# A decoder layer with 32 experts on one core: ScalarE's instructions of the expert loop put into the order in which they are written

## The chip, the core and the metric

The kernel runs on one core of one Trainium2 chip. The metric is device time in microseconds (us) of one execution. Its engines are TensorE (PE; its weight loads are PEld), VectorE (DVE), ScalarE (ACT), GpSimd (POOL) and SyncE (SP), each with an instruction stream of its own; they meet at semaphores. Transfers are issued here by SP (weights, plain loads and stores) and by POOL (indirect gathers and scatters).

## What is computed

One layer over 16 learned tokens and 512 input tokens of width 1024: two mixers in parallel (attention and a state-space scan), gated and added to the residual, then a mixture of 32 experts with a width of 256, of which every token uses two, and a last norm. All is float32. The change lies in the expert part alone:

```python
comb = jnp.sum(jax.nn.one_hot(ids, N_EXPERTS) * w[..., None], axis=1)     # two experts a token
for gi in range(N_EXPERT_GROUPS):
    h = silu(einsum('td,edf->tef', vt, w_gate[sl])) * einsum('td,edf->tef', vt, w_up[sl])
    out = out + einsum('tef,te,efd->td', h, comb[:, sl], w_down[sl])
return rmsnorm(h + out, norm_final)[:, N_META:]
```

## The kernel before

Everything up to about 577 us makes the mixers, the residual `h2` and the routing. Every expert has 64 places for tokens; two experts make a pair `p`, 0 to 15, which fills the 128 rows of TensorE. The expert loop (L1585 on) does for each pair, in the words of the code:

- `expert_gu(p)`: 32 matmuls (L1492) of the gathered tokens `xT` with gate and up weights into one PSUM tile `gu`, then on ScalarE the tanh `th` (L1495), on VectorE two products into `hp`;
- `load_gu`: SP issues the gate and up weights of pair p+3 in four transfers of 1,024 KB (L1038). There are six buffers, one an expert;
- `turn_x(p+1)`: TensorE turns the next pair's gathered rows, VectorE scales them, POOL issues the gather of pair p+4 into `xg` (L1393);
- `expert_h(p)`: TensorE turns `hp`, ScalarE copies it to `hT` (L1508);
- `y_mm`: 16 matmuls (L1528) with the down weights into two PSUM tiles `y`, and `y_split(p, hh)`, one for each half `hh` of the width;
- `load_dn`: SP issues the down weights of later experts (L1047).

`y_split` has two forms. For p below `NP` = 13, ScalarE scales each half of `y` into an SBUF tile `ys` (L1535), and behind the second half POOL scatters the rows of `ys` to a table `yd` in DRAM (L1537). There are two such tiles, used in turn: `ys` of pair p is written over `ys` of pair p-2, so it waits for the landing of that pair's scatter. Each scatter also waits for the landing of the scatter before it, since both write `yd`. For the last three pairs (13, 14, 15) there is no scatter. ScalarE and VectorE cut `y` into a high part `yh` (L1541) and a low part `yl` (L1542), and `combine(p, hh)` adds them to the right tokens with matmuls (L1559). `yh` and `yl` of pair 13 lie in the two tiles of `ys`: `yh` takes that of pair 12, `yl` that of pair 11.

The end of the loop is written out by hand: `combine(13, 0)` stands right behind `y_split(13, 1)` and ahead of `expert_gu(14)` on TensorE. After pair 13's weights, SP issues the last down weights in halves, the gain of the last norm, and eight loads (`load_y`, L1577) that fetch the scattered table `yd` back. POOL adds its two parts (`add_y`, L1580), VectorE adds them to `h2` (L1581), and `sum_h2` (L1569) adds `h2` into the PSUM sums of token blocks 2 and 3.

What sets the order: the program is written out by a scheduler that may move an instruction of an engine past others where the data allow it. `in_order(...)` (L68 on) ties each instruction of the engines that it names to the one before it on the same engine, so these run as written. In the expert loop it names VectorE, TensorE, POOL and SP. ScalarE is left to the scheduler. SP's transfers count on eight completion semaphores in turn, so that each waits for the landing of the transfer eight before it.

Of the kernel before, what the change touches and what calls it, by code (L numbers as in the profile page):

```python
# [72 lines left out]
def hybrid_layer(ctx: ExitStack, tc, A, out):  # L73
    nc = tc.nc
    act, dve, pool, pe = nc.scalar, nc.vector, nc.gpsimd, nc.tensor
# [17 lines left out]
    @contextmanager  # L93
    def in_order(*engines):

        traced = nc.cur_bb.bb.instructions
        n = len(traced)
        yield
        prev = {}
        for i in traced[n:]:  # L100
            if any(i.engine == e.engine for e in engines):
                k = str(i.engine)
                if k in prev:
                    tc.add_manual_dep(i, prev[k], mybir.DependencyInfo(mybir.DependencyClass.NoSync,
                                                                       mybir.DependencyReason.DATA), reason="in_order")
                prev[k] = i.name
# [917 lines left out]
    def load_gu(e, parts=(0, 1)):  # L1024

        if e >= NE:
            return
        i = e % NR
        w = GU_AT[i]
        if i in gus:  # L1030
            pass
        elif w == "u":
            gus[i] = btile(f"gu{i}", n=T)
        else:
            gus[i] = mws[w].tile([128, 4096], F32, tag=f"gu{i}", name=f"gu{i}", bufs=1).rearrange("p (k n) -> p k n", k=KD)
        for h in parts:
            k = slice(h * 4, h * 4 + 4)
            nc.sync.dma_start(gus[i][:, k], A["moe_gu"][e].rearrange("p (k n) -> p k n", k=KD)[:, k])  # L1038
# [419 lines left out]
    def turn_x(p, hh):  # L1458
        if p > 15:
            return  # L1460
        if hh == 0:
            xT[p] = ev.tile([128, KD, 128], F32, tag="xT", name="xT", bufs=1)
        t = xT[p]
        pt = ps("pxT")
        for k in range(4):
            pe.transpose(pt[:, k * 128:(k + 1) * 128], xgs[p % NX][:, (hh * 4 + k) * 128:(hh * 4 + k + 1) * 128], ident)  # L1466
        kk = slice(hh * 4, hh * 4 + 4)
        dve.tensor_mul(t[:, kk], pt.rearrange("p (k n) -> p k n", k=4),  # L1468
                       g_ffn[:, kk, None].to_broadcast([128, 4, 128]))
        if hh == 0:  # L1470
            return
        rh = xgs[p % NX][:, D:D + 1]
        dve.tensor_copy(rsl[:, p:p + 1], rh)
        dve.scalar_tensor_tensor(wsl[:, p:p + 1], wsl[:, p:p + 1], rh, rh, op0=ALU.mult, op1=ALU.mult)
        if p + NX < 16:
            gather(p + NX)

    def expert_gu(p):

        nf = 1 if p < 15 else 2  # L1480
        gu = [ps("gu") for _ in range(nf)]
        th, hp = (ev.tile([128, 256], F32, tag=x, name=x, bufs=n) for x, n in (("th", 1), ("hp", 2)))
        h_[p] = hp
        n = 256 // nf
        for kh in range(2):
            for f in range(nf):
                for k in range(kh * 4, kh * 4 + 4):
                    for e in range(2):
                        r, w = slice(e * 64, (e + 1) * 64), gus[(2 * p + e) % NR][:, k]
                        if nf > 1:  # L1490
                            w = w.rearrange("p (g f n) -> p g f n", g=2, f=nf)[:, :, f]
                        pe.matmul(gu[f][r, :2 * n], xT[p][:, k, r], w, start=(k == 0), stop=(k == KD - 1), skip_group_check=True)  # L1492
                if kh:
                    c = slice(f * n, (f + 1) * n)
                    act.activation(th[:, c], gu[f][:, :n], AF.Tanh, scale=rsl[:, p:p + 1])  # L1495
                    dve.scalar_tensor_tensor(hp[:, c], th[:, c], 1.0, gu[f][:, :n], op0=ALU.add, op1=ALU.mult)  # L1496
                    dve.tensor_mul(hp[:, c], hp[:, c], gu[f][:, n:2 * n])
# [3 lines left out]
    def expert_h(p, fs=(0, 1)):  # L1501
        if 0 in fs:
            hT_[p] = ev.tile([128, 2, 128], F32, tag="hT", name="hT", bufs=1)
        pt = ps("phT")
        for f in fs:
            pe.transpose(pt[:, f * 128:(f + 1) * 128], h_[p][:, f * 128:(f + 1) * 128], ident)
        c = slice(fs[0] * 128, (fs[-1] + 1) * 128)
        act.activation(hT_[p].rearrange("p f n -> p (f n)")[:, c], pt[:, c], AF.Copy)  # L1508

    def y_start(p):  # L1510
        if p < NP:
            y_[p] = ev.tile([128, D], F32, tag="y" + "hl"[p % 2], name="ys", bufs=1)
            return
        if p < 15:
            st = rx.tile([128, T], F32R, tag="rx", name="st")
            r = [ev.tile([128, D], F32R, tag="y" + x, name="y" + x, bufs=1) for x in "hl"]
        else:
            st, *r = (mo.tile([128, D + 1], F32R, tag=f"xg{i}", name=f"yx{i}", bufs=1)[:, :n] for i, n in enumerate((T, D, D)))
        dve.tensor_scalar(st, iot, tokf[:, p:p + 1], None, op0=ALU.is_equal)
        y_[p] = st, *r  # L1520
# [3 lines left out]
    def y_mm(p, f, hh):  # L1524
        if f == 0:
            yp[hh] = ps("y")
        for e in range(2):
            pe.matmul(yp[hh][e * 64:(e + 1) * 64], hT_[p][:, f, e * 64:(e + 1) * 64],  # L1528
                      dns[(2 * p + e) % ND][:, f, hh * 512:(hh + 1) * 512],
                      start=(f == 0), stop=(f == 1), skip_group_check=True)  # L1530
# [17 lines left out]
    def combine(p, hh, blocks=range(4)):  # L1548

        st, yh_, yl_ = y_[p]  # L1550
        c = slice(hh * 512, (hh + 1) * 512)
        for b in blocks:
            kept = b in HB
            on = kept and p > NP or p == 15 and hh
            if kept and p == NP:
                hs[b, hh] = ps("pcl")
            pc = hs[b, hh] if kept else more[b, hh] if on else ps("pc")
            for n, x in enumerate((yh_, yl_)):
                pe.matmul(pc, st[:, b * 128:(b + 1) * 128], x[:, c], start=(n == 0 and not on),  # L1559
                          stop=(n == 1 and (p == 15 or not kept and p < 15 - hh)), skip_group_check=True)  # L1560
            if not kept and p < 15 - hh:
                dve.tensor_add(h2[:, b, c], h2[:, b, c], pc)
            elif not kept:
                more[b, hh] = pc
# [17 lines left out]

    LC = [slice(0, 512), slice(512, 1024)]

    with in_order(dve, pe, pool, nc.sync):  # L1585
        for hh in range(2):
            turn_x(0, hh)
        for p in range(16):
            expert_gu(p)
            for h in range(2):  # L1590
                for e in range(2 * p + NR, 2 * p + NR + 2):
                    load_gu(e, (h,))
            if p < 15:
                turn_x(p + 1, 0)
                turn_x(p + 1, 1)
                if p > NP:
                    combine(p - 1, 1, range(CB))
                expert_h(p)
                if p > NP:
                    combine(p - 1, 1, range(CB, 4))  # L1600
                y_start(p)
                for hh in range(2):
                    for f in range(2):
                        y_mm(p, f, hh)
                    y_split(p, hh)
            else:
                y_start(p)
                add_y(2)
                add_y(3)
                expert_h(p, (0,))  # L1610
                combine(p - 1, 1, (2, 3))
                y_mm(p, 0, 0)
                expert_h(p, (1,))
                y_mm(p, 0, 1)
                for hh in range(2):
                    y_mm(p, 1, hh)
                    y_split(p, hh)
                combine(p - 1, 1, (0, 1))
                sum_h2()
                add_y(0)  # L1620
                add_y(1)
            for e in range(2 * p + ND, min(2 * p + ND + 2, 30)):
                load_dn(e)
            if 2 * p + ND + 1 in (31, 32):
                for c in LC:
                    load_dn(30, [c])
                    load_dn(31, [c])
                nc.sync.dma_start(dns[25 % ND][:, 0], bcast_row(A["g_fin"], D))
            if p == NP:
                for b in (2, 3, 0, 1):  # L1630
                    load_y(b)
            if NP <= p < 15:
                combine(p, 0)
        for b, hh in ((2, 0), (3, 0), (2, 1), (0, 0), (3, 1), (0, 1), (1, 0), (1, 1)):
            combine(15, hh, (b,))
# [181 lines left out]
```

## Time and profile before

| | us |
|---|---|
| three runs, median (lowest to highest) | 854.13 (851.97 to 854.8) |
| the profiled execution | 855.57 |
| its span, first to last instruction | 853.7 |
| TensorE busy | 774.0 |
| VectorE, ScalarE, POOL busy | 412.9, 275.9, 160.6 |

The profiled execution is 1.44 us above the median, and 1.87 us of its time lie outside the span. A row of a timeline gives the start, the duration, the engine, the line, the operation with output and inputs, how many instructions are merged in it (x), and in brackets how long the engine had been idle before and what ended that. Names are those of the program without their numbers. Sums of busy time are averages over stages with different limits; the expert loop is the stretch from 577 us to about 843 us.

### The profile page before, as it was taken

Reading aid. Unit: us, or ns where it says so; the run is one execution under the profiler, and the core shown is the slowest. Engines: PE = TensorE matmul, PEld = TensorE weight load, DVE = VectorE, ACT = ScalarE, POOL = GpSimd, SP = SyncE. Lnnn points to the kernel's source line nnn. Section 1 sums busy time; section 2 is a strip of 40 time slices with the busy share of each in tenths; the row PEclk is TensorE's granted clock in tenths of the full one; section 3 lists DMA queues with packets and bytes.
Section 4 is the critical chain, followed back from the end, with each engine's and each line's share of the span. In section 5 each row is a group of like instructions: output and inputs, shape, how many; then the busy total and the mean of one; then the engine's idle time right before and its main releaser. Section 6 shows DMA issues by size and latency. Waiting matters only on the chain.

```text
span 853.7 us, 11153 instructions
## 1 busy us (share of the span) xinstructions
PE 774.0 (91%) x4122; PEld 523.4 (61%) x4122; DVE 412.9 (48%) x945; ACT 275.9 (32%) x525; POOL 160.6 (19%) x201
## 2 busy tenths in 40 slices
PE   4999999999999999999999999959898887887494
PEld 4999886777788778767665788843333332332252
DVE  4787349865357545666857654261212211121155
ACT  6455333333135542455553424111111100011014
POOL 6100105322011000034435000051111010010042
PEclk9999999999999999999999999978999999999698
DMA  7721234324212241102122955869999999999932
GB/s 279 269 100 57 94 135 137 124 87 162 77 59 99 74 160 59 41 26 63 34 83 92 398 215 187 334 224 220 418 417 420 420 420 421 418 420 418 347 120 99
DMA packets 44445, 175.57 MB, mean 206 GB/s; under 512 B 9776, under 2 KB 14144, under 8 KB 28256
## 3 DMA queue, kind: packets, MB, share of 16 engines
q1 hardware_dynamic: 37808, 160.88, 49.9%
q0 software_dynamic: 5760, 13.71, 4.7%
q8 instruction: 35, 0.57, 0.3%
q10 hardware_dynamic: 816, 0.20, 0.1%
q14 instruction: 26, 0.21, 0.1%
HBM read 163.63 MB, written 15.27 MB: 210 GB/s over the span
## 4 chain that ended last, share of the span: by engine, by line
PE 67%; issue 11%; DMA 10%; DVE 6%; ACT 4%; POOL 0%; POOLq 0%; ACTq 0%; DVEq 0%
DMA yd<-ys,dst 8%; PE gu L1492 6%; PE y L1528 3%; PE pbr L676 3%; PE pbr L674 3%; PE pbr L673 3%; PE po L876 2%; PE ga L241 2%; PE gs L241 2%; PE ga L243 2%; PE ga L242 2%; PE gs L242 2%; PE pout L1093 2%; PE gs L243 2%; PE z L241 2%
## 5 line engine op out<-in xcount | busy, mean ns | idle before, releaser
L1492 PE MATMUL gu<-gu,xT 128*64 128x512 f32 (+1 forms) x544 | 129.7, 599 | 8.8 <-DMA gu<-in_moe_gu_dram 8.6
L1492 PEld LDWEIGHTS gu<-gu,xT 128*64 128x64 f32 x544 | 43.1, 143 | 92.0 <-issue 71.8
L1496 DVE SCALAR_TENSOR_TENSOR hp<-th,gu 128x256 f32<-128x256 f32 (+1 forms) x17 | 6.9, 405 | 188.0 <-ACT th L1495 188.0
L1495 ACT ACTIVATE th<-gu,rsl 128x256 f32<-128x256 f32 (+1 forms) x17 | 7.9, 462 | 180.0 <-PE gu L1492 180.0
L1528 PE MATMUL y<-dn,hT 128*64 128x512 f32 x256 | 58.7, 599 | 7.4 <-ACT hT L1508 7.4
L822 DVE CUSTOM_DVE_ANT_0 sp<-sp,amask 128x144 f32<-128x144 f32 (+4 forms) x80 | 33.9, 459 | 18.0 <-PE sp L814 14.9
L1528 PEld LDWEIGHTS y<-dn,hT 128*64 128x64 f32 x256 | 16.9, 136 | 38.4 <-issue 27.0
L1537 POOL DMA_INDIRECT yd<-ys,dst x13 | 13.1, 1005 | 132.3 <-ACT ys L1535 124.1
L852 PE MATMUL st<-qs,kq 97*128 97x512 f32 (+4 forms) x80 | 28.6, 358 | 1.0 <-DVE kq L797 1.0
L1393 POOL DMA_INDIRECT xg<-vd,idx x16 | 16.3, 1019 | 61.3 <-DMA yd<-ys,dst 33.9
L1466 PEld LDWEIGHTS pxT<-cst,xg 128*128 128x128 f32 x128 | 14.4, 146 | 18.5 <-issue 14.4
L301 POOL TENSOR_TENSOR rfs<-rfm,mhalf 128x4 f32<-128x4 f32 (+1 forms) x5 | 7.6, 1521 | 92.6 <-DVE rfm L300 92.6
L882 POOL TENSOR_TENSOR pw<-pw 128x400 f32<-128x400 f32 x14 | 15.9, 1157 | 43.8 <-PE po L876 43.8
L1468 DVE TENSOR_TENSOR xT<-pxT,pv 128x512 f32<-128x512 f32 x32 | 20.6, 681 | 6.8 <-PE pxT L1466 6.7
L853 PE MATMUL st<-qs,kq 97*128 97x512 f32 (+4 forms) x80 | 23.6, 296 | 0.2 <-DMA qs<-rs 0.2
L1466 PE MATMUL pxT<-cst,xg 128*128 128x128 f32 x128 | 18.3, 289 | 5.8 <-DMA xg<-vd,idx 5.8
L394 DVE SCALAR_TENSOR_TENSOR cacc<-xp,cwh,cacc 128x528 f32<-128x528 f32 x30 | 22.9, 763 | 0.4
L854 PE MATMUL st<-qs,kq 97*128 97x512 f32 (+4 forms) x80 | 23.0, 295 | 0.0
L861 ACT ACTIVATE pw<-st 128x512 f32<-128x512 f32 (+1 forms) x32 | 16.7, 547 | 19.4 <-PE st L857 16.1
L1535 ACT ACTIVATE ys<-y,wsl 128x512 f32<-128x512 f32 x26 | 16.9, 686 | 15.5 <-PE y L1528 15.5
L583 DVE TENSOR_SCALAR lm<-lm,acs 128x128 f32<-128x128 f32 x64 | 19.2, 366 | 2.5 <-DMA lm<-acd 2.5
L882 POOL TENSOR_TENSOR pw<-pw,pb 128x272 f32<-128x272 f32 (+2 forms) x42 | 20.2, 512 | 0.0
(925 smaller groups left out, 2043.9 us busy)
## 6 DMA issues: line engine op xcount, KB each, us to landing
gu<-in_moe_gu_dram SPq DMA_DIRECT2D x64, 1024.0 KB, 22.0
dn<-in_moe_dn_dram SPq DMA_DIRECT2D x30, 1024.0 KB, 21.0
win<-in_win_dram SPq DMA_DIRECT2D x19, 1024.0 KB, 4.7
yd<-bd POOLq DMA_DIRECT2D x2, 2048.0 KB, 12.2
lm<-acd SPq DMA_DIRECT2D x16, 256.0 KB, 3.6
wbs<-in_wbs_dram SPq DMA_DIRECT2D x4, 1024.0 KB, 4.7
wba<-in_wba_dram SPq DMA_DIRECT2D x4, 1024.0 KB, 11.4
wo<-in_wout_dram SPq DMA_DIRECT2D x4, 1024.0 KB
```

The costliest lines, as they stand in the source:

```text
L241: pe.matmul(dst, ah, bh, start=(i == 0), stop=False)
L242: pe.matmul(dst, ah, bl, start=False, stop=False)
L243: pe.matmul(dst, al, bh, start=False, stop=(i == n - 1))
L673: pe.matmul(pb_, wh[:, k], oh[k], start=(k == 0), stop=False)
L674: pe.matmul(pb_, wh[:, k], ol[k], start=False, stop=False)
L676: pe.matmul(pb_, wl[:, k], oh[k], start=False, stop=(k == last))
L822: dve.tensor_tensor_reduce(s_, s_, amask[:, L - nk + n0:L - nk + n1], 1.0, -3.0e38, op0=ALU.add, op1=ALU.max, accum_out=mx[:, n_:n_ + 1])
L852: pe.matmul(d_, kh_[0:97, kb], qh_[0:97, q0:q1], start=True, stop=False)
L882: last_sum[0] = eng.tensor_tensor(x, x, P[b], op=ALU.add)
L1466: pe.transpose(pt[:, k * 128:(k + 1) * 128], xgs[p % NX][:, (hh * 4 + k) * 128:(hh * 4 + k + 1) * 128], ident)
L1492: pe.matmul(gu[f][r, :2 * n], xT[p][:, k, r], w, start=(k == 0), stop=(k == KD - 1), skip_group_check=True)
L1528: pe.matmul(yp[hh][e * 64:(e + 1) * 64], hT_[p][:, f, e * 64:(e + 1) * 64], dns[(2 * p + e) % ND][:, f, hh * 512:(hh + 1) * 512], start=(f ...
```

## The change

The name `act` is added to the list of engines of the one `in_order` around the expert loop.

```diff
-    with in_order(dve, pe, pool, nc.sync):
+    with in_order(act, dve, pe, pool, nc.sync):
         for hh in range(2):
             turn_x(0, hh)
         for p in range(16):
```

Instructions of TensorE, VectorE, POOL and SP stand in the same order in both kernels. On ScalarE, the order is the same for pairs 0 to 4 and from `yh` of pair 13 on; between them the two `ys` of pairs 5 to 12 change places. The first place is ScalarE at pairs 5 to 7 (`th_6093`, `th_6160` and `th_6227` are the tanh of pairs 5, 6 and 7, `ys_6141` the output tile of pair 5), before:

```order
L1495 ACTIVATE th_6093<-gu_6092,rsl_5264 128x256
L1508 ACTIVATE hT_6136<-phT_6137 128x256
L1495 ACTIVATE th_6160<-gu_6159,rsl_5264 128x256
L1508 ACTIVATE hT_6203<-phT_6204 128x256
L1495 ACTIVATE th_6227<-gu_6226,rsl_5264 128x256
L1535 ACTIVATE ys_6141<-y_6142,wsl_5263 128x512
L1535 ACTIVATE ys_6141<-y_6148,wsl_5263 128x512
```

and now:

```order
L1495 ACTIVATE th_6093<-gu_6092,rsl_5264 128x256
L1508 ACTIVATE hT_6136<-phT_6137 128x256
L1535 ACTIVATE ys_6141<-y_6142,wsl_5263 128x512
L1535 ACTIVATE ys_6141<-y_6148,wsl_5263 128x512
L1495 ACTIVATE th_6160<-gu_6159,rsl_5264 128x256
L1508 ACTIVATE hT_6203<-phT_6204 128x256
```

The two `ys` of pair 5 moved from behind the tanh of pair 7 to behind `hT` of pair 5; the pairs 6 to 11 moved in the same way. The second place is ScalarE at pairs 11 to 13 (`ys_6543` and `ys_6606` are those of pairs 11 and 12, `th_6628`, `hT_6664` and `yh_6670` belong to pair 13), before:

```order
L1495 ACTIVATE th_6628<-gu_6627,rsl_5264 128x256
L1535 ACTIVATE ys_6543<-y_6544,wsl_5263 128x512
L1535 ACTIVATE ys_6543<-y_6550,wsl_5263 128x512
L1508 ACTIVATE hT_6664<-phT_6665 128x256
L1535 ACTIVATE ys_6606<-y_6607,wsl_5263 128x512
L1535 ACTIVATE ys_6606<-y_6613,wsl_5263 128x512
L1541 ACTIVATE yh_6670<-y_6673,wsl_5263 128x512
```

and now:

```order
L1535 ACTIVATE ys_6606<-y_6607,wsl_5263 128x512
L1535 ACTIVATE ys_6606<-y_6613,wsl_5263 128x512
L1495 ACTIVATE th_6628<-gu_6627,rsl_5264 128x256
L1508 ACTIVATE hT_6664<-phT_6665 128x256
L1541 ACTIVATE yh_6670<-y_6673,wsl_5263 128x512
```

Between the tanh of pair 13 and `yh` of pair 13 there stood the four `ys` of pairs 11 and 12; now there is `hT` alone, and all `ys` lie ahead.

## Rows read from the trace of the kernel before

**Rows 1.** Chain that ended last, in order of time: start, duration, engine or transfer.

```profile
783.04 8.41 DMA yd<-ys,dst
...
792.23 8.22 DMA yd<-ys,dst
```

**Rows 2.** Timeline of ScalarE in the expert loop.

```profile
646.61 0.69 ACT L1535 ACTIVATE ys<-y,wsl 128x512 f32<-128x512 f32 x1 [1.06 <-PE y L1528]
653.52 0.47 ACT L1495 ACTIVATE th<-gu,rsl 128x256 f32<-128x256 f32 x1 [6.23 <-PE gu L1492]
...
680.12 1.26 ACT L1535 ACTIVATE ys<-y,wsl 128x512 f32<-128x512 f32 x2
...
783.45 1.26 ACT L1535 ACTIVATE ys<-y,wsl 128x512 f32<-128x512 f32 x2
800.55 1.27 ACT L1541 ACTIVATE yh<-y,wsl 128x512 fp32r<-128x512 f32 x2 [15.84 <-DMA yd<-ys,dst]
813.70 0.47 ACT L1495 ACTIVATE th<-gu,rsl 128x256 f32<-128x256 f32 x1 [11.89 <-PE gu L1492]
```

**Rows 3.** Timeline of TensorE in the expert loop, matmuls alone.

```profile
646.36 7.04 PE L1492 MATMUL gu<-gu,xT 128*64 128x512 f32 x32
...
775.70 5.34 PE L1492 MATMUL gu<-gu,xT 128*64 128x512 f32 x14 [1.97 <-DMA gu<-in_moe_gu_dram]
...
783.61 3.65 PE L1528 MATMUL y<-dn,hT 128*64 128x512 f32 x16 [0.53 <-ACT hT L1508]
801.29 0.79 PE L1559 MATMUL pc<-yh,st 128*128 128x512 f32 x1 [14.03 <-ACT yh L1541]
...
805.42 8.23 PE L1492 MATMUL gu<-gu,xT 128*64 128x512 f32 x32
...
820.28 0.50 PE L1559 MATMUL pc<-yh,st 128*128 128x512 f32 x1
...
822.35 7.13 PE L1492 MATMUL gu<-gu,xT 128*64 128x256 f32 x64
...
835.63 3.60 PE L1569 MATMUL pcl<-h,cst 128*128 128x512 f32 x8
```

**Rows 4.** Timeline of POOL in the expert loop.

```profile
647.57 1.01 POOL L1537 DMA_INDIRECT yd<-ys,dst  x1 [2.63 <-ACT ys L1535]
...
681.66 1.00 POOL L1537 DMA_INDIRECT yd<-ys,dst  x1 [23.60 <-ACT ys L1535]
682.96 1.02 POOL L1393 DMA_INDIRECT xg<-vd,idx  x1 [0.30 <-issue]
...
792.23 0.98 POOL L1537 DMA_INDIRECT yd<-ys,dst  x1 [8.19 <-DMA yd<-ys,dst]
814.38 9.79 POOL L1580 TENSOR_TENSOR gu<-gu,gu 128x1024 f32<-128x1024 f32 x4 [21.16 <-PE pxT L1466]
```

**Rows 5.** Waits of SP's queue, at 791.5 to 792.5, then at 804 to 805.

```profile
SPq L1047 <- DMA gu<-in_moe_gu_dram: 2.7, 1, 2.7
...
SPq L1577 <- DMA gu<-in_moe_gu_dram: 1.8, 1, 1.8
```

**Rows 6.** Timeline of VectorE behind the last pair.

```profile
830.85 2.35 DVE L1581 TENSOR_TENSOR h<-h,gu 128x1024 f32<-128x1024 f32 x2
834.57 1.61 DVE L1542 SCALAR_TENSOR_TENSOR yx<-y,wsl,yx 128x512 fp32r<-128x512 f32 x2 [1.38 <-ACT yx L1541]
...
841.60 0.16 DVE L1655 SCALAR_TENSOR_TENSOR fq<-fq 128x1 f32<-128x1 f32 x1 [3.15 <-ACT gu L1651]
```

**Rows 7.** Stretches: length; PE, PEld, DVE, ACT, POOL busy; granted clock; DMA share; GB/s.

```profile
680.00:784.00 104.00, 87.44 (x358) 31.04 (x358) 15.68 (x43) 14.31 (x29) 13.07 (x13) 0.95 1.02 420
...
802.00:806.00 4.00, 3.94 (x10) 2.45 (x11) 2.12 (x4) 0.00 (x0) 0.00 (x0) 0.50 0.92 312
```

**Rows 8.** The page: POOL's queue (packets, MB, share) and its two plain blank fills.

```profile
q0 software_dynamic: 5760, 13.71, 4.7%
...
yd<-bd POOLq DMA_DIRECT2D x2, 2048.0 KB, 12.2
```

## The prediction

> **What bounds the kernel now.** I read the stretches first, then the chain that ended last, then the timelines of the engines around its longest step. From 680 to 784 us the transfers run at 420 GB/s with a DMA share of 1.02 [rows 7]: this part of the expert loop goes at the pace of the weights, and TensorE shows waits of some 2 us for them, as the 1.97 us ahead of the second half of pair 13's gate and up matmuls [rows 3]. A ScalarE that does the same work in another order can give nothing there. The end of the loop is different. TensorE finishes pair 13's `y` at 783.61 + 3.65 = 787.26 and then sits idle for 14.03 us, until 801.29, waiting for `yh` of ScalarE [rows 3]. No weight load is named there. ScalarE itself had been idle for 15.84 us, waiting for a scatter [rows 2], and the chain runs through two scatters in a row, 8.41 us from 783.04 and 8.22 us from 792.23 [rows 1]. The second could not start before the first had landed: POOL waited 8.19 us for it [rows 4]. Everything behind, to the end of the kernel, hangs on this.
>
> Why are two scatters left at 783? In the early pairs, ScalarE writes `ys` straight behind `y`: the second half of pair 4 at 646.61, its scatter leaves at 647.57 [rows 2, 4]. For pair 5 it waits behind the tanh of pair 7: 680.12, scatter at 681.66, and POOL had stood idle for 23.60 us, the gather behind it too, at 682.96 [rows 2, 4]. From there on, each scatter is about two pairs late, and no one notices, since nothing reads the table. At pair 13 someone does: `yh` and `yl` are written over the tiles of pairs 12 and 11, so all scatters must have landed. The two last ones, each late, now come one behind the other.
>
> **The change part by part.** (1) *Eight pairs of `ys` move up.* No work is added: 16 instructions keep their duration, 1.26 us a pair [rows 2]. In the new place they stand ahead of the next pair's tanh. That is a possible new wait: behind a `ys` that waits, tanh and `hT` queue on ScalarE, and behind those all of TensorE. The early pairs already have this order and show its cost. The second `ys` of pair 4 ends at 647.30, the next tanh starts at 653.52 because of TensorE, after 6.23 us of idleness [rows 2]. So the cost on the path is 0, hidden by seven microseconds of gate and up matmuls (7.04) [rows 3]; without that cover it would be 1.26 a pair, 10 us for eight.
>
> (2) *Eight scatters and the gathers behind them leave earlier*, by about 681.66 - (647.57 + 13.1) = 21 us at first; 13.1 is my estimate of the distance of two early pairs on TensorE (7.04 for gate and up, 3.65 for `y` [rows 3], some 2.4 for the turns and the two short waits between them). Their bytes do not change, but they move ahead of weights in a full pipe. POOL's queue moved 13.71 MB, of which the two blank fills are 4.2; the other 9.5 over 29 gathers and scatters give at most 0.33 MB each [rows 8], or 0.8 us at 420 GB/s [rows 7]. When pair 13's last weights land, two more scatters than before may have passed: 1.6 us. For pair 14's it is one, 0.8 us; for all that comes later none, the bytes are the same by then. The bounds are 0 and 1.6; I take 1.6, since the pipe is full.
>
> (3) *The wait of 14.03 us goes. What is late next?* Pair 13's `y` ends at 787.26 + 1.6 = 788.9. `yh` follows it at once, as for pair 14, where the matmuls of `combine` start at 820.28 and the next pair's at 822.35: 2.07 us [rows 3]. So pair 14's gate and up matmuls start at 790.9 instead of 805.42. Their weights: SP's transfer at 791.8 had waited for a landing of such weights, which is the last of pair 14's, since each transfer waits for the eighth before it [rows 5]; with the 0.8 it is 792.6, and the second half of the matmuls wants them at 790.9 + 3.5 = 794.4. They take 7.04 us as in the early pairs rather than 8.23 [rows 3], and end at 797.9 instead of 813.65: **15.75 us gained**. The 8.23 and the 4.13 us of `combine` (805.42 - 801.29) were run after the idle time, with a granted clock of 0.50, the lower level of 1.2 GHz, at 802 to 806 [rows 7]. If the clock is low again, these cost 1.19 + 2.06 = 3.3 us of the gain; I take the short ones, since TensorE works without a gap of that size now.
>
> (4) *The rest of the tail moves along, if its transfers are there.* Pair 15's matmuls start 8.70 us after pair 14's end (822.35 - 813.65 [rows 3]): 806.6. The last gate and up weights landed by 804.9 [rows 5]: no wait. `sum_h2` would come at 835.63 - 15.75 = 819.9 [rows 3]. It needs the fetched table, and these loads do not move, as they stand behind the weights on SP. POOL added them from 814.38 on, four in 9.79 us [rows 4]; the row names TensorE as what ended the wait, but those loads are issued after 802 and land about then, so I let POOL start at 814.4 again. Its second sum is ready at 819.3, VectorE's two adds (1.2 us each [rows 6]) at 820.5. The first two of the eight `sum_h2` matmuls (0.45 each) do without them and end at 820.8: just in time. The fourth sum is ready at 824.2, on VectorE at 825.4; the norm's first step, 841.60 before [rows 6], would want VectorE at 825.85. Both margins are under half a microsecond, so I take off 0.5: **15.3 us**.
>
> The profiled execution would go from 855.57 to 840.3; it lies 1.44 above the median of the runs shown, and from that median, 854.13, I get 838.8.
>
> **What the Trainium skill says on two of these steps.** On (1), "PSUM — Partial Sum Buffer", section "Engine vs sequencer instructions", says that ScalarE's queue is strictly first in, first out: a `ys` that waits for its scatter holds all behind it. The trace agrees: the `yh` at 800.55 held ScalarE for 15.84 us [rows 2]. By that rule alone, fixing the order can lose; it is the second rival. On (2), "DMA: Bandwidth & Descriptors", section "Issuing engines are not separate DMA queues", says that transfers of SP and POOL share the same 16 engines and interleave, so an earlier scatter is paid by weights; by that rule (2) is 1.6 us rather than 0, which the DMA share of 1.02 bears out [rows 7].
>
> **The rivals.** *The transfers hold the tail.* The gain of 15.3 uses nearly all the slack that the fetched table has. If its loads land 5 us later than before (SP issues them behind transfers that wait for landings of weights), POOL, VectorE and `sum_h2` move by 5, and the time is 843.3; with the low clock of (3) on top of a smaller slip it is about the same. Against it: the bytes ahead of them are the same by then, and one scatter less runs beside them. *ScalarE is held by its own order (slower).* `ys` of pair p needs the landing of pair p-2's scatter. From that issue (647.57 for pair 4) to `ys` two pairs later there are about 26 - 1.7 = 24 us, and 6.2 more until the tanh behind it would start. It decides once a scatter takes over 30 us from issue to landing: at 33 us, six pairs (7 to 12) lose 3.3 each, 20 us, and with the 15.3 won back the kernel ends near 859. Against it: scatters took 8.2 to 8.4 in the fullest stretch [rows 1]. *The wait stays.* If the last scatter lands near 800 whenever it is issued, because the weights crowd it out, the time is 854.1. Against it, the same 8.2 us.
>
> **How the numbers follow.** The forecast has 0.77, the late transfers 0.14, the wait that stays 0.05, the slower case 0.04. The likeliest is the forecast, 838.8. It spans 836.0 (no shift in (2), where the fetched table caps the gain at 16.2, less 2 us, as far as the lowest run lies below the median) to 842.1 (low clock); I carry the range to 845.0 to take in the late transfers. About 0.3%, 2.6 us, is what a measurement of this kernel can tell from no change: faster by more 0.91, within 0.05, slower 0.04.
>
> **What would show it.** Right: in the new timelines each second `ys` follows its `y` within a microsecond, all 13 scatters are issued before 772, `yh` of pair 13 waits for TensorE alone, the idle time ahead of pair 13's `combine` falls below 1 us, pair 14's tanh starts near 798, and POOL's sums still start near 814. Wrong: a `ys` that waits for a transfer, TensorE waiting for weights ahead of pair 14 or 15 for more than 2 us, or VectorE's adds ahead of `sum_h2` waiting for POOL. The forecast fails most easily at (4), at the fetched table.

## The result and the profile after

The changed kernel takes 844.58 us (median of 4 runs, 842.84 to 846.47), beside 853.40 for the kernel before (4 runs, 851.97 to 854.80; three of them are those of the table above). The ratio is 0.9897, with an interval of 0.9863 to 0.9931: it is 0.7 to 1.4% faster. The forecast was 838.8 with a range of 836.0 to 845.0. The time lies inside the range, at its far end: of the 15.3 us that were promised, about 9 came. The profiled execution took 846.47, its span 844.7 instead of 853.7: 9.0 us less. It is the longest of the four, but a second profile of this kernel (experiment 8, an execution of 844.43 us) shows the same wait at the end.

The big wait is gone. This is the timeline of ScalarE of the changed kernel around pair 13 (start, duration, engine, line, operation, count; in brackets the idle time before it and what ended it):

```profile
770.93 0.69 ACT L1535 ACTIVATE ys<-y,wsl 128x512 f32<-128x512 f32 x1 [2.06 <-PE y L1528]
772.65 0.69 ACT L1535 ACTIVATE ys<-y,wsl 128x512 f32<-128x512 f32 x1 [1.03 <-PE y L1528]
786.45 0.69 ACT L1541 ACTIVATE yh<-y,wsl 128x512 fp32r<-128x512 f32 x1 [2.09 <-PE y L1528]
797.51 0.47 ACT L1495 ACTIVATE th<-gu,rsl 128x256 f32<-128x256 f32 x1 [8.70 <-PE gu L1492]
```

The two `ys` of pair 12 end at 773.34, ten microseconds before the place where the last two stood in [rows 2], and `yh` of pair 13 waits for TensorE alone; in [rows 2] it waited 15.84 us for a scatter. The timeline of POOL:

```profile
660.03 1.00 POOL L1537 DMA_INDIRECT yd<-ys,dst  x1 [2.63 <-ACT ys L1535]
...
773.61 0.99 POOL L1537 DMA_INDIRECT yd<-ys,dst  x1 [16.49 <-ACT ys L1535]
...
815.61 11.41 POOL L1580 TENSOR_TENSOR gu<-gu,gu 128x1024 f32<-128x1024 f32 x4 [41.01 <-PE y L1528]
```

Pair 5's scatter leaves at 660.03, before at 681.66, and the last of the thirteen at 773.61, before at 792.23 [rows 4]. But look at the last row: the four sums of the fetched table take 11.41 us where they took 9.79. TensorE, matmuls alone, shows both what was won and what was given back:

```profile
784.42 3.65 PE L1528 MATMUL y<-dn,hT 128*64 128x512 f32 x16 [0.53 <-ACT hT L1508]
788.00 0.50 PE L1559 MATMUL pc<-yh,st 128*128 128x512 f32 x1
...
790.07 7.36 PE L1492 MATMUL gu<-gu,xT 128*64 128x512 f32 x32
...
806.13 7.13 PE L1492 MATMUL gu<-gu,xT 128*64 128x256 f32 x64
...
819.41 1.02 PE L1569 MATMUL pcl<-h,cst 128*128 128x512 f32 x2
824.87 5.35 PE L1569 MATMUL pcl<-h,cst 128*128 128x512 f32 x6 [4.43 <-DVE h L1581]
```

Pair 14's gate and up matmuls start at 790.07 instead of 805.42, pair 15's at 806.13 instead of 822.35, and `sum_h2` at 819.41 instead of 835.63 [rows 3]: 16.2 us won. Then comes a row that was not there before: six of the eight `sum_h2` matmuls wait 4.43 us for an add of VectorE, and take 5.35 us, where all eight took 3.60 [rows 3]. This wait stands in the chain that ended last (start, duration, engine, tile, line), where no POOL sum and no VectorE add of the fetched table stood before:

```profile
815.61 2.34 POOL gu L1580
...
818.04 3.41 POOL gu L1580
...
821.47 3.35 DVE h L1581
...
824.87 5.35 PE pcl L1569 x6
```

The account: 16.2 won up to `sum_h2`, of which 9.0 arrived in the span. The other 7.2 went between there and the norm. VectorE's first norm step (L1655) starts 5.97 us after the start of `sum_h2` in [rows 3] and [rows 6] (841.60 - 835.63), and now at

```profile
832.59 0.16 DVE L1655 SCALAR_TENSOR_TENSOR fq<-fq 128x1 f32<-128x1 f32 x1 [3.35 <-ACT gu L1651]
```

which is 13.18 us after it: 7.2 lost, 4.43 of them by the wait and 2.8 by the slower matmuls behind it. From the norm to the end of the span it is 12.1 us in both kernels.

### The profile page after: what moved, and what is told of

It reads as the page before. It is cut to its first block, busy times and chain, and to the rows that moved or that the text cites. A ratio compares the mean times of both kernels' runs of the same rounds, so it can differ in the third digit from the quotient of the medians.

```text
span 844.7 us, 11164 instructions
## 1 busy us (share of the span) xinstructions
PE 772.8 (91%) x4122; PEld 523.0 (62%) x4122; DVE 413.9 (49%) x945; ACT 277.6 (33%) x525; POOL 162.7 (19%) x201
## 4 chain that ended last, share of the span: by engine, by line
PE 71%; DMA 17%; DVE 5%; ACT 4%; issue 1%; POOL 1%; SPq 0%; ACTq 0%; DVEq 0%; POOLq 0%
DMA gu<-in_moe_gu_dram 11%; PE gu L1492 8%; PE y L1528 4%; DMA dn<-in_moe_dn_dram 3%; PE pbr L673 3%; PE pbr L676 3%; PE pbr L674 3%; PE po L876 2%; PE ga L241 2%; PE gs L241 2%; PE ga L243 2%; PE ga L242 2%; PE gs L242 2%; PE gs L243 2%; PE pout L1093 2%; PE pout L1094 2%
## 5 line engine op out<-in xcount | busy, mean ns | idle before, releaser
L1492 PE MATMUL gu<-gu,xT 128*64 128x512 f32 (+1 forms) x544 | 127.0, 585 | 10.9 <-DMA gu<-in_moe_gu_dram 10.9
```

## The experiments

**Theory.** The four last sums collide: POOL's sums and VectorE's adds work on tiles in the same memory at the same time and hold each other up, and through `sum_h2` this costs TensorE 4.4 us and some clock. **Rivals:** the fetched table itself comes too late for the early `sum_h2`; or the gain at pair 13 is smaller than read and the 7 us have another source. For the gain there is the theory that the wait for two late scatters was all there was to win, and the rival that the earlier scatters of all eight pairs have a worth or a price of their own.

**1. The changed kernel with POOL's sum of the fetched table moved to VectorE.** VectorE then does eight adds in a row, and none of them can meet one of POOL's.

```diff
     def add_y(b):
-        pool.tensor_tensor(ya[b, 0], ya[b, 0], ya[b, 1], op=ALU.add)
+        dve.tensor_add(ya[b, 0], ya[b, 0], ya[b, 1])
         dve.tensor_add(h2[:, b], h2[:, b], ya[b, 0])
```

> The changed kernel, with POOL's four sums of the fetched table moved to VectorE. Theory (POOL and VectorE slow each other when both add whole rows at once; that is what delays the second sum of h2): VectorE's adds take 1.2 us each again, the one that the sum of h2 waits for ends near 820.5 instead of 824.8, TensorE's wait of 4.4 us shrinks below 1 us, its clock stays up, and the time falls by 4 to 6 us below the changed kernel, to 838.5 to 841 (before: 853.4). Rival (the fetched table simply lands too late): the wait stays at 3 us or more and the time stays near 844.6.

It took 840.3 us (839.54 to 841.12, 4 runs), beside 855.01 for the kernel before: ratio 0.9819, interval 0.9803 to 0.9836. The intervals of this version and the changed kernel lie apart; it is the best of all here, and beats both kernels. Its VectorE:

```profile
816.77 1.23 DVE L1580 TENSOR_TENSOR gu<-gu,gu 128x1024 f32<-128x1024 f32 x1 [0.87 <-DMA gu<-yd]
818.03 1.23 DVE L1581 TENSOR_TENSOR h<-h,gu 128x1024 f32<-128x1024 f32 x1
819.20 1.23 DVE L1580 TENSOR_TENSOR gu<-gu,gu 128x1024 f32<-128x1024 f32 x1
820.46 1.23 DVE L1581 TENSOR_TENSOR h<-h,gu 128x1024 f32<-128x1024 f32 x1
```

and its TensorE:

```profile
820.60 3.98 PE L1569 MATMUL pcl<-h,cst 128*128 128x512 f32 x8
```

Every add takes 1.23 us, the one that POOL did in 2.4 included. The eight matmuls run in one piece, and TensorE needs 7.7 us from `sum_h2` to its last matmul, close to the 7.3 of before. The gain, 14.7 us by the medians and 15.5 by the ratio (855.01 times 0.0181), is about what the forecast had promised for the order alone.

**2. The changed kernel with the fetched table's loads issued ahead of the load of `g_fin`.**

```diff
                     load_dn(30, [c])
                     load_dn(31, [c])
-                nc.sync.dma_start(dns[25 % ND][:, 0], bcast_row(A["g_fin"], D))
             if p == NP:
                 for b in (2, 3, 0, 1):
                     load_y(b)
+                nc.sync.dma_start(dns[25 % ND][:, 0], bcast_row(A["g_fin"], D))
```

> The changed kernel, with the load of the last norm's gain issued behind the eight loads of the table instead of ahead of them; its issue took 4.05 us. Theory (late table plus collision): the first table loads are issued 4 us earlier, near 799, the fourth about 1.4 us earlier (it waits for a landing of weights), POOL's first sum starts near 812, TensorE's wait of 4.4 us falls to 2 or 3, the time to 841 to 843. Rival (the table's landing has no part in it, POOL is released by TensorE as its row says): POOL still starts at 815.6 and the time stays near 844.6.

It took 845.76 (844.45 to 845.96; ratio 0.9887, 0.987 to 0.9903), which can't be told from the changed kernel, and the edit mostly missed. On SP's queue of the changed kernel, then of this one:

```profile
799.09 4.05 SPq L1628 DMA_DIRECT2D dn<-in_g_fin_dram  x1
803.25 9.88 SPq L1577 DMA_DIRECT2D gu<-yd  x8
```

```profile
798.99 12.74 SPq L1577 DMA_DIRECT2D gu<-yd  x8
812.70 0.33 SPq L1631 DMA_DIRECT2D dn<-in_g_fin_dram  x1
```

The first of the eight loads is issued 4 us earlier, but the 4 us that the issue of `g_fin` took stayed at that place of the queue. The view of L1577 gives the shortest, the median and the longest of the eight issues in ns:

```profile
L1577 SPq DMA_DIRECT2D gu<-yd x8: 319/320/4002, 799.0 to 811.4; - x8
```

The longest, 4.0 us, is the first, so the second load leaves at 803.08; in the changed kernel none took over 0.52 us. Why an issue takes 4 us at that place was not looked into. POOL's first sum needs both of the first two loads. So it starts at 814.18 instead of near 812, between the 815.61 of the changed kernel's first profile and the 813.90 of its second (experiment 8):

```profile
814.18 11.49 POOL L1580 TENSOR_TENSOR gu<-gu,gu 128x1024 f32<-128x1024 f32 x4 [39.89 <-DMA gu<-yd]
```

This row names what ends POOL's wait, the landing of the table, where the rows of the changed kernel and [rows 4] name TensorE. The sums still take 11.49 us, VectorE's first two adds 6.67 where 2.35 would do [rows 6], and the matmuls of `sum_h2` still wait, 0.83 and 2.16 us:

```profile
816.79 6.67 DVE L1581 TENSOR_TENSOR h<-h,gu 128x1024 f32<-128x1024 f32 x2 [2.24 <-POOL gu L1580]
```

```profile
820.24 1.13 PE L1569 MATMUL pcl<-h,cst 128*128 128x512 f32 x2 [0.83 <-DVE h L1581]
...
823.52 4.54 PE L1569 MATMUL pcl<-h,cst 128*128 128x512 f32 x6 [2.16 <-DVE h L1581]
```

So the table has its part in the wait: TensorE was ready for `sum_h2` at 819.4 in both kernels, and POOL's start, 1.4 us earlier than in the first profile, took 1.4 us off the wait (2.99 in all instead of 4.43). The 3 us that are left are there although POOL starts where the forecast had it. What a table that is there 5 us earlier would do stays untried.

**3. The kernel before with ScalarE tied to program order from pair 11 on.** The late scatters of pairs 5 to 8 stay late; only those of the end move.

```diff
+        tied = ExitStack()
         for p in range(16):
+            if p == 11:
+                tied.enter_context(in_order(act))
...
+        tied.close()
```

> The kernel before, with ScalarE tied to its written order only from pair 11 on; pairs 5 to 10 keep their late output copies. Theory (the whole gain is the wait at pair 13): as the changed kernel, 843 to 846, no idle time of 14 us ahead of pair 13's combine. Rival (earlier scatters and gathers along the loop help too): less than half of the gain, 849 or more.

It took 846.91 (844.6 to 848.19; ratio 0.9904, 0.9885 to 0.9924): 0.9 us above the expected span, but by its ratio, 0.9904 beside 0.9897, the whole gain of the change as far as the intervals can tell. Its POOL,

```profile
681.78 1.00 POOL L1537 DMA_INDIRECT yd<-ys,dst  x1 [23.59 <-ACT ys L1535]
...
775.12 0.99 POOL L1537 DMA_INDIRECT yd<-ys,dst  x1 [8.38 <-DMA yd<-ys,dst]
```

is late at pair 5 as in [rows 4] and 17 us ahead of [rows 4] at pair 12 (775.12, before 792.23). What the change does to pairs 5 to 8 has no worth and no price that can be measured here.

**4. The kernel before with tiles of their own for pair 13's `yh` and `yl`.** The order stays, and the scatters stay late; what goes is the reason to wait for them, since these two tiles are now those of gathered rows that are no longer needed.

```diff
-            r = [ev.tile([128, D], F32R, tag="y" + x, name="y" + x, bufs=1) for x in "hl"]
+            r = [mo.tile([128, D + 1], F32R, tag=f"xg{i}", name=f"yg{i}", bufs=1)[:, :D] for i in (1, 2)] if p == NP else [ev.tile([128, D], F32R, tag="y" + x, name="y" + x, bufs=1) for x in "hl"]
```

> The kernel before, ScalarE's order untouched, with the high and low parts of pair 13 in two gather tiles that are free by then instead of the tiles of the output copies: pair 13 no longer waits for the scatters of pairs 11 and 12. Theory (the wait for the scatters is the cause, the order only what made them late): combine of pair 13 starts near 788 with the scatters as late as before (issued near 783 and 792), and the time is that of the changed kernel, 843 to 846. Rival (late scatters cost in another way too, for example as they hold back the table's loads): 848 or more.

It took 846.6 (845.22 to 847.96; ratio 0.989, 0.987 to 0.9911): the same gain once more. Its scatters are as late as before, and its `combine` does not care:

```profile
783.61 1.00 POOL L1537 DMA_INDIRECT yd<-ys,dst  x1 [14.49 <-ACT ys L1535]
792.77 1.00 POOL L1537 DMA_INDIRECT yd<-ys,dst  x1 [8.16 <-DMA yd<-ys,dst]
```

```profile
787.76 1.19 PE L1559 MATMUL pc<-yg,st 128*128 128x512 f32 x4
```

Here too `sum_h2` waits 4.45 us for VectorE, so that wait belongs to the earlier tail, and not to ScalarE's order.

**5. The kernel before with the sums on VectorE**, the edit of experiment 1 without the change.

> The kernel before, ScalarE's order untouched, with POOL's four sums of the fetched table moved to VectorE. Theory (the collision of POOL and VectorE exists only where the tail has moved up on them; before, POOL had ended at 824.2 and VectorE began at 830.85): nothing to win here, VectorE takes 4.9 us for the first two blocks instead of 2.35, all hidden or up to 1.5 us lost, ratio to before 0.999 to 1.002. Rival (VectorE is simply the better engine for these sums, whatever the order): a gain of 3 us or more here too, ratio 0.996 or less.

855.63 us (852.43 to 857.3, 10 runs) beside 856.04 for the kernel before: ratio 1.0 (0.9975 to 1.0025), nothing. Its TensorE still waits at pair 13:

```profile
802.89 0.79 PE L1559 MATMUL pc<-yh,st 128*128 128x512 f32 x1 [14.07 <-ACT yh L1541]
```

The collision of the sums costs nothing as long as the tail comes 16 us later. Each of the two edits was looked at alone: the order gives about 9 us, the sums 0, and both together about 15.

**6. The changed kernel with one tile for `ys` in place of two**, so that each `ys` needs the landing of the scatter just before it. This halves the room of the slower rival.

```diff
-            y_[p] = ev.tile([128, D], F32, tag="y" + "hl"[p % 2], name="ys", bufs=1)
+            y_[p] = ev.tile([128, D], F32, tag="y" + "h", name="ys", bufs=1)
```

> The changed kernel, with one tile for the output copies instead of two, so that each waits for the scatter of the pair just before it. Theory (the written order has room: a scatter lands 8.4 us after its issue, and the next pair's copy comes at least 12 us after it): no copy waits for a scatter, time as the changed kernel, 842 to 847. Rival (ScalarE is held by its own order as soon as the room shrinks): copies wait for landings, tanh and TensorE behind them, 850 or more.

846.95 us (843.34 to 848.31; ratio 0.9895, 0.9841 to 0.9949), as the changed kernel. All 26 waits of `ys` are for TensorE, none for a scatter; the row (waiting instruction, releaser: us in all, times, longest) reads the same in both:

```profile
ACT ys L1535 <- PE y L1528: 40.2, 26, 2.2
```

**7. The changed kernel, where POOL and VectorE take turns once.** POOL's third sum is written over the tile that VectorE's second add reads, and so starts only when that add is done. Nothing else changes; POOL's first and second sums stand as they were.

```diff
-        pool.tensor_tensor(ya[b, 0], ya[b, 0], ya[b, 1], op=ALU.add)
-        dve.tensor_add(h2[:, b], h2[:, b], ya[b, 0])
+        o = ya[b or 3, 0]; pool.tensor_tensor(o, ya[b, 0], ya[b, 1], op=ALU.add)
+        dve.tensor_add(h2[:, b], h2[:, b], o)
```

> The changed kernel, with POOL's third sum (block 0) made to wait until VectorE's add of block 3 is done, by writing it over a buffer that this add reads. Theory (POOL and VectorE cannot run these two-input operations at the same time, the later one waits for the whole of the earlier one): VectorE's add of block 3 takes 1.2 us instead of 3.35, TensorE's wait falls from 4.4 to about 2.3 us, the time by 1 to 3 us below the changed kernel, ratio about 0.002 lower. POOL's second sum stays stretched to 3.4 us, since it still meets VectorE's add of block 2. Rival (VectorE's add is slow there for another reason, such as the fetched rows landing at that time): it stays at 3 us or more, the time too.

**8. The changed kernel again**, beside 7 on the same chip.

> The changed kernel itself, beside the others on the same chip, for the comparison: ratio to before about 0.990, TensorE idle for some 4.4 us ahead of the sum of h2, VectorE's add of block 3 near 3.35 us.

VectorE's two adds in the changed kernel, in the first profile:

```profile
818.00 1.22 DVE L1581 TENSOR_TENSOR h<-h,gu 128x1024 f32<-128x1024 f32 x1 [3.28 <-POOL gu L1580]
821.47 3.34 DVE L1581 TENSOR_TENSOR h<-h,gu 128x1024 f32<-128x1024 f32 x1 [2.25 <-POOL gu L1580]
```

the second of them in experiment 8, and TensorE's wait for it there:

```profile
819.75 3.35 DVE L1581 TENSOR_TENSOR h<-h,gu 128x1024 f32<-128x1024 f32 x1 [2.23 <-POOL gu L1580]
```

```profile
823.15 5.02 PE L1569 MATMUL pcl<-h,cst 128*128 128x512 f32 x6 [4.45 <-DVE h L1581]
```

and both in experiment 7, where POOL waits (then its rows on POOL):

```profile
817.50 1.22 DVE L1581 TENSOR_TENSOR h<-h,gu 128x1024 f32<-128x1024 f32 x1 [3.28 <-POOL gu L1580]
820.96 1.23 DVE L1581 TENSOR_TENSOR h<-h,gu 128x1024 f32<-128x1024 f32 x1 [2.24 <-POOL gu L1580]
```

```profile
815.11 5.81 POOL L1580 TENSOR_TENSOR gu<-gu,gu 128x1024 f32<-128x1024 f32 x2 [39.30 <-PE y L1528]
822.26 4.71 POOL L1580 TENSOR_TENSOR gu<-gu,gu 128x1024 f32<-128x1024 f32 x2 [1.34 <-DVE h L1581]
```

The second add falls from 3.35 to 1.23 as soon as POOL's third sum does not start with it. That settles the collision: same operation, tiles and data, another neighbour. TensorE's wait falls from 4.45 to 2.31 us:

```profile
822.24 2.84 PE L1569 MATMUL pcl<-h,cst 128*128 128x512 f32 x6 [2.31 <-DVE h L1581]
```

POOL's second sum meets VectorE's first add as before and stays long: 5.81 us for the first two sums. And the collision has moved: VectorE's third add now meets POOL's fourth sum, so the last two adds take 4.54 us, where the changed kernel has 3.19 and [rows 6] 2.35:

```profile
824.65 4.54 DVE L1581 TENSOR_TENSOR h<-h,gu 128x1024 f32<-128x1024 f32 x2 [1.15 <-POOL gu L1580]
```

The norm's first step follows on them at 829.11, so a part of what TensorE won is lost again.

In time, 7 took 844.28 (842.48 to 846.77; ratio 0.9875, 0.9835 to 0.9915) and 8 took 846.48 (844.43 to 848.15; ratio 0.9902, 0.9863 to 0.994), over 6 runs each. The difference of 2 us has the expected sign, but the intervals overlap: the traces show the mechanism, but the times can't tell these two kernels apart.

## Why the prediction came out half right

**Step (1), the `ys` move at no cost: right.** All 26 waits of `ys` are for TensorE, and none is over 2.2 us. ScalarE's fixed order did no harm, since no `ys` waited for a transfer. The slower rival is refuted, also with half the room (experiment 6). (Its price was summed wrongly, without effect: beyond 24 + 6.2 us, a scatter of 33 us costs 2.8 a pair, 17 in all, not 3.3 and 20.)

**Step (2), up to 1.6 us on pair 13's weights: not shown either way.** Pair 13's `y` ends at 788.07, 0.8 us later than before, but the end differs by more than that between executions: 786.33 in the changed kernel's second profile, and 788.81 in experiment 5, which has the old order. (The 0.33 MB of this step is a mean of 29 transfers, not a bound.) One scatter was issued later than I said, 773.61 instead of before 772, which had no effect.

**Step (3), 15.75 us: right.** Pair 14's matmuls start at 790.07 (forecast 790.9) and its tanh at 797.51 (798); the matmuls end 16.2 us earlier than before. Experiments 3 and 4 show the cause apart from the rest: the wait for two late scatters. Moving only the last `ys`, or leaving all of them late and taking the shared tiles away, each gives what the whole change gives. The low clock that I had weighed against this step did not come; the stretch of the changed kernel (length; PE, PEld, DVE, ACT, POOL busy; granted clock; DMA share; GB/s) where [rows 7] show 0.50 reads 1.00, and behind it come the two in which the time was lost:

```profile
784.00:802.00 18.00, 17.58 (x82) 8.71 (x84) 7.62 (x17) 2.60 (x5) 0.00 (x0) 1.00 0.95 379
...
819.40:824.80 5.40, 1.03 (x3) 0.20 (x2) 3.33 (x2) 0.00 (x0) 5.40 (x3) 0.84 0.12 47
824.80:833.90 9.10, 9.04 (x22) 5.01 (x22) 5.21 (x8) 2.53 (x8) 3.17 (x3) 0.72 0.01 2
```

**Step (4), the tail moves along: this is the one that failed.** `sum_h2` started at 819.41, as forecast (819.9). The term that was wrong is "VectorE's two adds (1.2 us each) at 820.5 ... just in time": the second add ended at 824.81. The 4.3 us between are 1.2 because POOL started later (815.61 instead of 814.38), 1.0 because its second sum took 3.41 us instead of 2.4, and 2.1 because VectorE's second add took 3.34 instead of 1.2. So the larger part, 3.1 us, is the collision, and it was not among the rivals: there the tail was held by a late table. Of the signs that I had named for a wrong forecast, one came: VectorE's adds wait for POOL. Experiment 2 shows that the collision stays when POOL starts at 814.18, as I had it: TensorE then still waits 0.83 + 2.16 us, close to these 3.1. Its 0.83 also shows a reading that was wrong: the first two `sum_h2` matmuls do not "do without" VectorE's adds, they need the first of the two. On the wait follow slower matmuls: 5.35 us for six, at a granted clock of 0.72 in the stretch, so that the higher level of 2.4 GHz was not granted throughout. Of the forecast 15.3 us, this took 7.2; against that stand 0.5 that I had taken off at (4) and 0.5 that (2) and (3) cost less than I took.

The mistake was to price two engines' adds each by its duration when the other was not at work, [rows 4] 9.79 / 4 = 2.45 and [rows 6] 2.35 / 2 = 1.2, for a place where they overlap. Before, POOL had finished at 824.17, and VectorE began at 830.85: they never met on these lines. The sign was in the trace of before all the same. VectorE's L1519 there reads

```profile
817.91 1.56 DVE L1519 TENSOR_SCALAR st<-iot,tokf 128x512 fp32r<-128x512 f32 x1
...
830.45 0.48 DVE L1519 TENSOR_SCALAR yx<-iot,tokf 128x512 fp32r<-128x512 f32 x1
```

1.56 us while POOL was at its sums, and 0.48 us when it was done: one line with two durations. Experiment 5 has the old order and no sums on POOL, and there the first of these, at the same place, takes 0.48 us too:

```profile
818.50 0.48 DVE L1519 TENSOR_SCALAR st<-iot,tokf 128x512 fp32r<-128x512 f32 x1
```

So the 1.08 us came with POOL's sums; that they come about in the same way as those of the adds is not shown. The Trainium skill states the rule for the adds, in "SBUF — State Buffer", section "SBUF: two separate sides": a VectorE instruction with two inputs in that memory and a GpSimd instruction that reads it share a pair of ports, and whichever starts first holds it for its whole instruction, while the other stands still. The traces agree: 3.34 us is 1.2 and 2.1 of standing still behind a sum of 2.3 that began with it; POOL's 3.41 is 2.4 and 1.0 behind an add of 1.22. With turns (experiment 7) VectorE's standing still is gone at this add, and with one engine (experiment 1) both are.

**The range** held by luck: its width was meant for a late table, and the time that came is near that rival's 843.3 for another reason. A tail that moves along freely was to give 15.3 us; experiment 1, where it does, gave about that (14.7 by the medians, 15.5 by the ratio).

**What stays open.** POOL started 1.2 us later in the changed kernel's first profile, and so did the table: SP's first load of it left at 803.25 there, and POOL's first sum came 12.4 us behind it. The same distance stands in the kernel before (801.93 to 814.38) and in experiment 8 (801.51 to 813.90); SP in the kernel before, then SP and POOL in experiment 8:

```profile
801.93 9.96 SPq L1577 DMA_DIRECT2D gu<-yd  x8
```

```profile
801.51 9.92 SPq L1577 DMA_DIRECT2D gu<-yd  x8
```

```profile
813.90 11.40 POOL L1580 TENSOR_TENSOR gu<-gu,gu 128x1024 f32<-128x1024 f32 x4 [41.07 <-DMA gu<-yd]
```

Why the loads leave at a different time in two executions of one kernel, by 1.7 us here, was not settled.

## What to carry to other kernels

A copy that nobody waits for can be late for eight rounds at no cost, and then all its lateness is due at once, at the first instruction that writes over its tiles: look for it at the last round of a loop, and cure either the order or the shared tile. Before you count on a tail that moves up, list which engines will then work at the same time and did not before, and price their instructions by rows in which they overlap; a line that shows two durations in the trace tells where to look. Two edits can be worth 9 and 0 alone and 15 together, so the second bottleneck is worth an experiment on both versions.

## What the runs showed of the hardware that I had not expected

- An add of VectorE with two inputs (128x1024 f32) takes 1.22 us, and 3.34 to 3.35 when a sum of POOL starts with it; POOL's sum takes 2.34, and 3.41 when it starts just behind VectorE's add. For these adds POOL was no help: VectorE does both of a block in 2.46 us, about as long as POOL takes for one.
- Eight scatters issued 19 to 27 us earlier into the fullest stretch moved the end of pair 13's `y` by no more than it differs between executions (787.26 and 788.81 with the old order, 788.07 and 786.33 with the new).
- Some 4 us of SP's issuing belonged to a place in its queue and not to a transfer: the issue of `g_fin` took 4.05 us there and 0.33 us behind the table's loads, and the load that came into its place took 4.00.
- After a wait of 4.43 us TensorE ran on at a granted clock of 0.72 over the next 9 us. After experiment 2's 0.83 and 2.16 us, its six matmuls were slow too (4.54 us; the clock at 823.5 to 832 is 0.80). After experiment 7's 2.31 us they were not (2.84 us), and the stretch that holds them (columns as above) reads 0.98:

```profile
822.00:832.00 10.00, 6.56 (x22) 4.07 (x22) 8.84 (x12) 3.84 (x12) 7.37 (x6) 0.98 0.05 18
```

What decides between these is not settled by these runs.
